# Word order behind the heads' products, and two steps that change places

## The chip, the cores and the metric

The kernel runs on one core of one Trainium2 chip. The metric is device time in microseconds of that core, first to last, of one execution; lower is better. A run's time is the median of several executions. A profile is one further execution, recorded by the hardware profiler.

The core has a matrix engine (TensorE, PE in the profile; its weight loads are shown as PEld), VectorE (DVE), ScalarE (ACT), GpSimd (POOL) and SyncE (SP). Each runs its own list of instructions in the order in which they were written, and waits for the others by semaphores. DMAs are issued here from SP and POOL.

## The reference

One layer of a decoder: normalise the rows of x, project them to q, k, v and a gate, do stick-breaking attention with 32 heads, gate, project back, add x, normalise again. `SEQ` is 256 rows, `D_MODEL` 4096, in float32.

```python
xn = rms_norm(h, norm_attn)
proj = xn @ w_in                      # (256, 4096) @ (4096, 16384)
q, k, v, g = split(proj, 4)
z = q @ k.T / sqrt(128)               # per head, strictly causal
log_a = log_sigmoid(z) + suffix_sum(log_sigmoid(-z))
o = exp(log_a) @ v
h = h + (o * silu(g)) @ w_out         # (256, 4096) @ (4096, 4096)
out = rms_norm(h, final_norm)
```

The two projections are nearly all of the arithmetic, and they read 320 MB of weights.

## The kernel before

**Products in three parts.** A float32 number is split into a high and a low part that TensorE can take; a product of two such matrices is then three matmuls, high by high, high by low, low by high, all into one PSUM bank. Such a *triple* is what `mm3` issues: 128 x 128 stationary by 128 x 512 moving, three times. The high part of a weight is a copy on ACT (`wh` in the profile), the low part is the difference on DVE (`wl`).

**Units and steps.** The work is cut into 20 *units*: 0 to 15 for the input projection (each gives the columns of two heads), 16 to 19 for the output projection. A unit has 16 *steps*; a step takes 256 of the 4096 inputs, two raw weight tiles of 512 KB loaded by SP.

**Eight or seven products.** A step is a 2 x 2 by 2 x 2 block product. Units 0 and 16 are plain, of eight triples a step. In the others a step has either eight triples (`EIGHT_PARTS`) or, by a scheme of the Strassen kind, seven (`SEVEN_PARTS`). A step of seven needs sums of weight blocks: POOL issues two accumulating DMAs for one of them (`add_block`), and DVE makes the others in place (`sums`: rows `raw<-raw,raw` and `raw<-raw`), before ACT and DVE split the results. In the profile a step of eight gives DVE two operations `wl<-raw,wh` of 128 x 1024; a step of seven three of these, one `wh<-raw,wh` of 128 x 512 and three sums. The low part of the third part of a step of seven (part 2, counted from 0) can be made only after the sums.

Which steps are of seven is in two lists:

```python
SEVEN = (1, 2, 4, 5, 7, 8, 10, 11, 13, 14)      # units 1 to 15
SEVEN_OUT = (1, 2, 4, 5, 7, 10, 11, 13, 14)     # units 17 to 19
```

In the last unit, 19, steps 11, 13 and 14 are of eight in any case, and its order is 0, 1, 3, 2, 4, 6, 5, 13, 7, 9, 8, 14, 10, 11, 12, 15. The stationary side has forms to match, built once (`new_forms`, `sums_of`, `blocks_of_heads`): six or seven blocks for the units 17 to 19, from the heads' outputs, which are read back from DRAM (`p<-spill`) for the steps of seven.

**Heads.** While a unit of the input projection runs, the two heads of the unit before are computed: transposes, scores, a scan by a triangular matrix, and the product with v. These are small matmuls, issued in bursts by `ten` between the triples (ten bursts a unit; tiles `tr`, `z`, `o`). `ten` sets a counter, `since_others`, to zero; each triple adds one.

**The order of the words.** `mm3` lets the 512 columns of a matmul be read and written in an order other than 0 to 511: four rounds, and in each every fourth group of columns, groups of eight words ("e") or of four ("c"). It is the same arithmetic. Three letters give the orders of a triple's matmuls. The seven triples behind a burst take theirs from `BEHIND_OTHERS`; after those, the first triple of a step takes `cce` (even steps) or `ecc` (odd), and all others `eee`.

**The last units.** In units 17 to 19 DVE and ACT also finish the blocks of the unit before: `block_out` loads a piece of x, adds it (`h<-h,xres`, DVE), squares the sum (`sq<-h`, ACT; this is an activation and a second instruction that reads its accumulated sum), and multiplies by the final norm's weights (`h<-h,grow`, DVE, in `gain_on`). There are four such pieces a unit.

**What sets the order.** No order is written by hand. `Plan` runs every piece of work through a list of planned events: a request for an engine has a cost and a key (a due time, in PE's time: `place_at`, `first`), and whenever an engine is free in the plan, the waiting request with the lowest key is written next. An engine is never left idle in the plan when something is ready. What is written is then fixed: on the chip each engine follows it. The wrapper's one line calls every instruction, so that the profile gives nearly all of them line 131, and tiles tell them apart.

Of the kernel before, what the change touches and what calls it, by code (L numbers as in the profile page):

```python
# [33 lines left out]

ROUNDS = 4
RUNS = {"e": 8, "c": 4}
BEHIND_OTHERS = ("ccc", "ecc", "eee", "cce", "eee", "eee", "ecc")
IN_STEP = ("cce", "ecc")
WARM, IDLE = 10, 640

# [3 lines left out]


SEVEN = (1, 2, 4, 5, 7, 8, 10, 11, 13, 14)
SEVEN_OUT = (1, 2, 4, 5, 7, 10, 11, 13, 14)
SOONER = 1.5
LATE, LATE_ADD = 1600, 2200
RAW_BUFS = 7  # L50
# [12 lines left out]
HEADS_AHEAD = 0  # L63
SUMS_LATER = 2
H_LATER = 6
ON_SCALAR = ((1, 3, 5), (1, 3))
AHEAD, SUMS_AHEAD = 6.0, 3.0
BLOCKS_LATER = 2
# [179 lines left out]
def kernel(  # L248
# [41 lines left out]
    for u, (kind, w, cols) in enumerate(units):  # L290
        for s in (step_at(u, k) for k in range(NS)):
# [3 lines left out]
            else:  # L295
                which = SEVEN_PARTS if s in (SEVEN if u < OUT0 else SEVEN_OUT) and not (u == LAST and s in EIGHT_LAST) else EIGHT_PARTS
            for i, (k, place, prods) in enumerate(which):
# [23 lines left out]
    def place_at(u, s):  # L321

        return place_of[u + int(s // NS), step_at(u + int(s // NS), int(s % NS))]
# [5 lines left out]
    def dve(emit, n, key=None, more=0, **kw):  # L329
        n = n if isinstance(n, tuple) else (n,)  # L330
        cost = sum(vector_ns(m) for m in n) + 122 * (len(n) - 1) + more
        return nc.work("vector", cost, emit, soon() if key is None else key, **kw)

    def act(emit, n, key=None, **kw):
        n = n if isinstance(n, tuple) else (n,)
        cost = sum(scalar_ns(m) for m in n) + 100 * (len(n) - 1)
        return nc.work("scalar", cost, emit, soon() if key is None else key, **kw)
# [169 lines left out]
    def new_forms(i, what):  # L507
        n = len(SEVEN_FORMS if i in (SEVEN if what == "s" else SEVEN_OUT) else EIGHT_FORMS)
        h = sp.tile([P, n, P], F32R, tag=f"xh{i}", name=f"{what}h{i}")
        l = sp.tile([P, n, P], F32R, tag=f"xl{i}", name=f"{what}l{i}")  # L510
        forms[i] = h, l
        return h, l
# [7 lines left out]
    def differences(i, y, key):  # L520

        y4 = y.rearrange("p (a b) c -> p a b c", a=KT)
        yield dve(
            lambda: nc.vector.tensor_tensor(
                out=y4[:, :, 0, :], in0=y4[:, :, 0, :], in1=y4[:, :, 1, :], op=ALU.subtract
            ),
            2 * P, key,
        )
        yield from both_parts(i, slice(4, 6), y4[:, :, 0, :], key)

    def sums_of(i, y, what, key):

        tt = nc.vector.tensor_tensor
        if i not in (SEVEN if what == "n" else SEVEN_OUT):
            yield from differences(i, y, key)
# [418 lines left out]
    def blocks_of_heads(s):  # L954
# [11 lines left out]
        key = min(place_at(OUT0, s + SUMS_LATER), place_of[OUT0 + 1, s] - 3e3)  # L966
        if s in SEVEN_OUT and s < NS - 1:
            nc.give("gh")
# [54 lines left out]
    def load_out(c, t):  # L1023
        pool, tag, bufs = (sp, "x" + "hl"[t] + str(LAST_STEPS[c - NJ + 4]), 1) if c >= NJ - 2 else (wp, "gh", ROWS)
        xres[c, t] = pool.tile([P, W], F32, tag=tag, name=f"xres{c}_{t}", bufs=bufs)
        return moved(
            "sync", lambda: nc.sync.dma_start(xres[c, t], x[t * P : (t + 1) * P, c * W : (c + 1) * W]), [W], soon(),
            after=lambda: nc.tell(("xres", c, t)),
        )

    def load_gain(c):
        grow[c] = wp.tile([P, W], F32, tag="gh", name=f"grow{c}", bufs=ROWS)
        return moved(
            "sync", lambda: nc.sync.dma_start(grow[c], gain_out[:, c * W : (c + 1) * W].partition_broadcast(P)), [W],
            soon(), after=lambda: nc.tell(("grow", c)),
        )

    def squares(c, t, place, cut, key=None):

        junk = att.tile([P, cut.stop - cut.start], F32, tag="att", name=f"sq{c}_{t}_{cut.start}")  # L1040
        yield act(
            lambda: nc.scalar.activation(
                junk, hs[c, t][:, cut], AF.Square, accum_out=ssq_h[:, t, place : place + 1]
            ),
            cut.stop - cut.start, key and key - 1e3,
        )

    ALL = slice(0, W)
# [1 line left out]
    def gain_on(c, t, key=None):  # L1050
        h = hs[c, t]
        yield nc.until(("grow", c))
        yield dve(lambda: nc.vector.tensor_tensor(out=h, in0=h, in1=grow[c], op=ALU.mult), W, key)

    def block_out(c, t, key):

        h = hs[c, t]
        yield nc.take("gh")
        yield load_out(c, t)
        yield nc.until(("xres", c, t))  # L1060
        yield nc.take("att")
        yield dve(lambda: nc.vector.tensor_tensor(out=h, in0=h, in1=xres[c, t], op=ALU.add), W, key)
        nc.give("gh")
        yield from squares(c, t, c, ALL, key)
        nc.give("att")
        yield from gain_on(c, t, key)

    def blocks_out(u, c):

        for d in range(2):  # L1070
            for t in range(NT):
                yield nc.until(("used", u, step_at(u, 2 * (NT * d + t))), ("C", u - 1))
                if t == 0:
                    yield nc.take("gh")
                    yield load_gain(c + d)
                key = place_at(u, 2 * (NT * d + t) + H_LATER)
                yield from block_out(c + d, t, key)
            nc.give("gh")
            nc.tell(("h", c + d))
# [74 lines left out]
    def part_done(c, t, place, cut, late):  # L1154
        yield nc.take("att")
        yield from squares(c, t, place, cut, late)
        nc.give("att")
        if place == NJ - 2:
            yield dve(lambda: mean_before_last(t), (NJ * NT, 64), late)
            nc.tell(("mean", t))  # L1160
        elif place == NJ - 1:
            yield nc.until(("mean", t))
            yield dve(lambda: joined(t), 64, late - 2)
            nc.tell(("most", t))
        else:
            yield nc.until(("most", t))
            yield from finish(c, t, late)
# [36 lines left out]
    def rows_out(c, t, f, key):  # L1204
        h = hs[c, t]
        if c >= NJ - 2:
# [6 lines left out]
            )  # L1213
        elif c in ON_SCALAR[t]:
            yield act(lambda: nc.scalar.activation(h, h, AF.Copy, scale=f), W, key)
# [21 lines left out]
    def product(n, k):  # L1237
# [4 lines left out]
        orders = "eee"  # L1242
        if since_others < len(BEHIND_OTHERS):
            orders = BEHIND_OTHERS[since_others]
        elif p["i"] == 0 and k == 0:
# [91 lines left out]
```

## Time and profile before

| | us |
|---|---|
| median of 3 runs | 1709.23 |
| lowest, highest | 1705.84, 1709.48 |
| profiled execution | 1706.34 |
| its span, first to last instruction | 1704.6 |
| granted TensorE clock, mean | 0.997 |

A page of a profile gives the busy time of each engine, the chain of work that ended last, the costliest groups of instructions, and DMA issues. A row of a timeline has the start, the length, the engine, the operation with what it writes and reads, and in brackets the idle time before it and what ended that. PE's matmuls are pipelined, so their lengths overlap; what counts is the distance from one start to the next. In a table of stretches a row has the length, then busy time and number of instructions of PE, PEld, DVE, ACT and POOL, the granted clock, the DMA engines' share and GB/s.

The stationary high parts of the input and output projections are `sh` and `oh`, the low ones `sl` and `ol`. A triple is `wh` by high, `wl` by high, `wh` by low.

### The profile page before, as it was taken

What the parts mean: (1) busy time and instruction counts of PE and PEld (TensorE: products, weight loads), DVE (VectorE), ACT (ScalarE), POOL (GpSimd) and SP (SyncE); (2) the same over time, 40 slices, a digit from 0 to 9 for tenths busy, and PEclk for the clock granted to TensorE, in tenths of its full rate; (3) what the DMA queues carried; (4) which work ended last, traced back from release to release, by engine and by line L of the source; (5) the groups of instructions that cost most, each with busy time, mean ns of one, the idle gap of its engine ahead of it and who ended that gap; (6) DMA issues with size and microseconds to landing.
All of it is one profiled execution on the core that took longest, in us unless ns stands there. A gap on an engine that the chain in (4) does not pass through costs nothing.

```text
span 1704.6 us, 25109 instructions
## 1 busy us (share of the span) xinstructions
PE 1685.6 (99%) x7776; PEld 1415.9 (83%) x7776; DVE 1607.4 (94%) x2025; ACT 1202.5 (71%) x1633; POOL 325.0 (19%) x400
## 2 busy tenths in 40 slices
PE   9999999999999999999999999999999999999996
PEld 7888888888888888888888888888888888888785
DVE  8889999999999999999999999999999977999997
ACT  8986767676767676767676768686767765666664
POOL 0012222222222222221212121212122112122110
PEclk9999999999999999999999999999999999999998
DMA  9968887979797878797978797878788977889795
GB/s 348 329 197 246 231 245 220 255 212 256 208 269 196 269 197 272 195 279 195 268 204 261 208 256 213 254 216 248 220 243 224 295 244 241 240 251 284 218 293 187
DMA packets 248439, 412.78 MB, mean 242 GB/s; under 512 B 28016, under 2 KB 72560, under 8 KB 248304
## 3 DMA queue, kind: packets, MB, share of 16 engines
q1 hardware_dynamic: 194544, 354.24, 62.2%
q0 software_dynamic: 53472, 56.65, 20.5%
q8 instruction: 61, 1.00, 0.2%
q14 instruction: 74, 0.61, 0.1%
q10 hardware_dynamic: 288, 0.28, 0.0%
HBM read 402.93 MB, written 8.13 MB: 241 GB/s over the span
## 4 chain that ended last, share of the span: by engine, by line
PE 94%; DVE 3%; issue 1%; DMA 1%; ACT 0%; SPq 0%; DVEq 0%; ACTq 0%
PE acc L131 90%; PE z L131 2%; PE o L131 2%; DVE wl L131 1%; PE tr L131 1%; DVE h L131 0%; DVE raw L131 0%; ACT wh L131 0%; DMA raw<-in_w_in_dram 0%; DMA raw<-in_w_out_dram 0%; DMA xres<-in_x_dram 0%; DVE wh L131 0%; DVE gv_sb L131 0%; SPq L131 0%; DVE scalars L131 0%
## 5 line engine op out<-in xcount | busy, mean ns | idle before, releaser
L131 ACT CAST wh<-raw 128x1024 fp32r<-128x1024 f32 (+1 forms) x989 | 918.2, 969 | 370.8 <-DVE raw L131 166.8
L131 DVE TENSOR_TENSOR wl<-raw,wh 128x1024 fp32r<-128x1024 f32 (+1 forms) x815 | 974.9, 1219 | 56.4 <-ACT wh L131 25.1
L131 PE MATMUL acc<-wh,sh 128*128 128x512 f32 x2048 | 774.3, 390 | 0.3 <-DVE sh L131 0.3
L131 PE MATMUL acc<-wh,sl 128*128 128x512 f32 x1898 | 727.9, 383 | 1.2 <-DVE sl L131 1.2
L131 PE MATMUL acc<-wl,sh 128*128 128x512 f32 x1748 | 669.0, 383 | 0.2 <-DVE wl L131 0.2
L131 POOL DMA_DIRECT2D raw<-in_w_in_dram x300 | 258.6, 957 | 1026.7 <-DMA raw<-in_w_in_dram 424.2
L131 PEld LDWEIGHTS acc<-wh,sh 128*128 128x128 f32 x2048 | 384.1, 188 | 78.0 <-PE acc L131 4.8
L131 PEld LDWEIGHTS acc<-wh,sl 128*128 128x128 f32 x1898 | 355.8, 187 | 67.2 <-DVE sl L131 1.8
L131 PEld LDWEIGHTS acc<-wl,sh 128*128 128x128 f32 x1748 | 328.3, 188 | 54.8 <-DVE wl L131 0.5
L131 DVE TENSOR_TENSOR raw<-raw,raw 128x512 f32<-128x512 f32 x348 | 237.5, 686 | 6.0 <-DMA raw<-in_w_out_dram 2.1
L131 PE MATMUL acc<-wh,oh 128*128 128x512 f32 x512 | 192.6, 384 | 0.6 <-DVE gv_sb L131 0.6
L131 PE MATMUL acc<-wh,ol 128*128 128x512 f32 x488 | 186.7, 383 | 0.0
L131 PE MATMUL acc<-wl,oh 128*128 128x512 f32 x464 | 177.7, 383 | 2.6 <-DVE wl L131 2.6
L131 DVE TENSOR_TENSOR wh<-raw,wh 128x512 fp32r<-128x512 f32 x174 | 119.3, 686 | 1.6 <-ACT wh L131 1.5
L131 DVE TENSOR_TENSOR raw<-raw 128x512 f32<-128x512 f32 x174 | 119.0, 684 | 0.0
L131 PEld LDWEIGHTS acc<-wh,oh 128*128 128x128 f32 x512 | 95.9, 187 | 18.0 <-DVE gv_sb L131 0.9
L131 PEld LDWEIGHTS acc<-wh,ol 128*128 128x128 f32 x488 | 91.5, 187 | 16.4
L131 PEld LDWEIGHTS acc<-wl,oh 128*128 128x128 f32 x464 | 87.0, 187 | 19.3 <-DVE wl L131 3.8
L131 POOL DMA_DIRECT2D raw<-in_w_out_dram x48 | 41.5, 968 | 181.4 <-DMA raw<-in_w_out_dram 78.7
L131 ACT ACTIVATE f<-f 128x384 f32<-128x384 f32 x96 | 50.5, 526 | 3.0
L131 POOL DMA_DIRECT2D p<-spill x27 | 17.5, 692 | 86.5 <-DVE ol L131 44.1
L131 DVE SCALAR_TENSOR_TENSOR gv_sb<-acc,scalars,gv_sb 128x512 f32<-128x512 f32 x45 | 33.5, 744 | 0.0
(83 smaller groups left out, 755.4 us busy)
## 6 DMA issues: line engine op xcount, KB each, us to landing
raw<-in_w_in_dram SPq DMA_DIRECT2D x1024, 256.0 KB, 4.3
raw<-in_w_out_dram SPq DMA_DIRECT2D x256, 256.0 KB, 4.5
raw<-in_w_in_dram POOLq DMA_DIRECT2D x300, 128.0 KB, 5.1
p<-spill POOLq DMA_DIRECT2D x27, 256.0 KB, 4.5
raw<-in_w_out_dram POOLq DMA_DIRECT2D x48, 128.0 KB, 5.1
xr<-in_x_dram SPq DMA_DIRECT2D x16, 256.0 KB, 5.5
xres<-in_x_dram SPq DMA_DIRECT2D x16, 256.0 KB, 6.2
out_dram<-h SPq DMA_DIRECT2D x16, 256.0 KB, 2.8
```

Of the source, the lines that this page charges most:

```text
L131: return self.tc.keep_in_program_order(getattr(self.engine, name)(*args, **kw))
```

## The change

Four edits.

- `BEHIND_OTHERS`: triples four and seven behind a burst. The fourth goes from `cce` to `eee`, the seventh from `ecc` to `cce`. Triples one (`ccc`), two (`ecc`), three, five and six (`eee`) stay.
- `SEVEN_OUT`: in units 17 to 19 step 4 becomes one of eight products, step 8 one of seven. The number of steps of each kind stays. With the steps go the form of the stationary blocks of steps 4 and 8, the accumulating DMAs, and the second reading of a step's heads' outputs.
- `GAIN_LATER`: the multiplication by the final norm's weights in `block_out` gets a key that is 8 us later. The last block pair, which multiplies in another place, isn't touched.
- `squares`: the planner's cost of a square is now that of two operations, of the piece's columns and of 64, instead of one. The instruction is the same.

```diff
-BEHIND_OTHERS = ("ccc", "ecc", "eee", "cce", "eee", "eee", "ecc")
+BEHIND_OTHERS = ("ccc", "ecc", "eee", "eee", "eee", "eee", "cce")
...
-SEVEN_OUT = (1, 2, 4, 5, 7, 10, 11, 13, 14)
+SEVEN_OUT = (1, 2, 5, 7, 8, 10, 11, 13, 14)
...
+GAIN_LATER = 8.0
...
             lambda: nc.scalar.activation(
                 junk, hs[c, t][:, cut], AF.Square, accum_out=ssq_h[:, t, place : place + 1]
             ),
-            cut.stop - cut.start, key and key - 1e3,
+            (cut.stop - cut.start, 64), key and key - 1e3,
         )
...
         yield from squares(c, t, c, ALL, key)
         nc.give("att")
-        yield from gain_on(c, t, key)
+        yield from gain_on(c, t, key + GAIN_LATER * 1e3)
```

## The prediction

> **What bounds the kernel.** I read the page first, then the three last units as stretches of time, then the timeline of TensorE (PE), then that of VectorE (DVE) before each place where PE stood still.
>
> ```profile
> span 1704.6 us, 25109 instructions
> PE 1685.6 (99%) x7776; PEld 1415.9 (83%) x7776; DVE 1607.4 (94%) x2025; ACT 1202.5 (71%) x1633; POOL 325.0 (19%) x400
> PE 94%; DVE 3%; issue 1%; DMA 1%; ACT 0%; SPq 0%; DVEq 0%; ACTq 0%
> ```
>
> PE has work in 99% of the span and carries 94% of the chain that ended last, so a change counts only if it shortens PE's row: by an idle stretch, or by the spacing of its 7158 matmuls of 512 columns. DVE at 94% is next, and is late first.
>
> ```profile
> 1449.80:1528.40 78.60, 78.60 (x358) 66.86 (x357) 75.90 (x93) 50.56 (x64) 13.79 (x16) 1.00 0.84 253
> 1528.40:1610.30 81.90, 79.58 (x359) 66.77 (x358) 78.46 (x94) 50.08 (x64) 16.65 (x20) 1.00 0.87 253
> 1610.30:1691.90 81.60, 81.10 (x367) 68.28 (x365) 72.62 (x100) 46.98 (x65) 7.45 (x9) 1.00 0.68 219
> ```
>
> These are units 17, 18 and 19 (length, then PE's busy time and instructions, then the other engines; PE's clock is 1.00). Units 17 and 18 hold the same 119 products, but 18 takes 3.3 us more and PE idles 2.3 us in it; in unit 19 it idles 0.5 us. PE's timeline has the places:
>
> ```profile
> 1554.85 0.40 PE L131 MATMUL acc<-wh,oh 128*128 128x512 f32 x1
> 1555.49 0.50 PE L131 MATMUL acc<-wl,oh 128*128 128x512 f32 x1 [0.24 <-DVE wl L131]
> 1555.83 0.40 PE L131 MATMUL acc<-wh,ol 128*128 128x512 f32 x1
> ...
> 1585.26 0.40 PE L131 MATMUL acc<-wh,oh 128*128 128x512 f32 x1
> 1587.74 0.49 PE L131 MATMUL acc<-wl,oh 128*128 128x512 f32 x1 [2.08 <-DVE wl L131]
> ...
> 1632.12 0.39 PE L131 MATMUL acc<-wh,oh 128*128 128x512 f32 x1
> 1632.77 0.48 PE L131 MATMUL acc<-wl,oh 128*128 128x512 f32 x1 [0.26 <-DVE wl L131]
> ```
>
> Starts are what to compare; undisturbed matmuls start 0.22 us apart (below). The first place is step 5 of unit 18 (0.64 + 0.34 - 0.44 = 0.54 us lost), the second step 11 of unit 18 (2.48 - 0.22, and some 0.1 at the next matmul as at the first place: 2.37), the third step 4 of unit 19 (0.65 - 0.22 + 0.1: 0.53). Together 3.44 us. All three are steps of seven products waiting for `wl` of a part that DVE makes from sums; the first and third follow a step of seven directly, and in the second a norm weight is multiplied just ahead of the sums.
>
> **Steps 4 and 8.** What a step costs DVE, from the groups of units 17 and 18, and the accumulating loads' landing time from the page:
>
> ```profile
> L131 DVE TENSOR_TENSOR wl<-raw,wh 128x1024 fp32r<-128x1024 f32 x79 | 92.6, 1218 | 1.7 <-ACT wh L131 1.5
> L131 DVE TENSOR_TENSOR raw<-raw,raw 128x512 f32<-128x512 f32 x34 | 23.2, 686 | 1.5 <-DMA raw<-in_w_out_dram 1.3
> L131 DVE TENSOR_TENSOR raw<-raw 128x512 f32<-128x512 f32 x17 | 11.6, 684 | 0.0
> L131 DVE TENSOR_TENSOR wh<-raw,wh 128x512 fp32r<-128x512 f32 x17 | 11.6, 684 | 0.9 <-ACT wh L131 0.9
> L131 DVE TENSOR_TENSOR h<-h,grow 128x512 f32<-128x512 f32 x8 | 5.5, 686 | 1.6 <-ACT sq L131 1.6
> raw<-in_w_out_dram POOLq DMA_DIRECT2D x48, 128.0 KB, 5.1
> ```
>
> A step of seven takes DVE 3 x 1.22 + 2 x 0.69 + 2 x 0.68 = 6.4 us and PE 7 x 3 x 0.22 = 4.62 us: DVE falls 1.8 us behind. A step of eight takes DVE 2 x 1.22 = 2.44 us and PE 5.28 us: DVE gains 2.84 us. The count of both kinds stays, so do the products, the accumulating loads of POOL's queue, SP's loads and the reloads of the heads' outputs; they move from step 4 to step 8. The forms are built in unit 16, where PE waits for none of this; I put them at 0.
>
> In unit 18 step 5 then follows two steps of eight (3 and 4) instead of a step of seven, so DVE has 1.8 + 2.84 = 4.6 us more before it, and it lacked 0.54: all of that goes. In unit 19, in its order 0, 1, 3, 2, 4, 6, 5, 13, 7, 9, 8, step 4 becomes one of eight itself and the stall of 0.53 has no place left; step 8 lies between steps 9 and 14, both of eight. In units 17 and 18 step 8 now follows step 7, a pair of sevens as 1 and 2 are. What is late next is DVE at steps 8 and 11 there. Ends: 0, and 1.8 + 2.84 = 4.6 us a unit if no lead is left. I take 0: unit 17 has four such pairs in its 78.60 us and PE never idles, and the 4.6 us that step 4 no longer takes lies ahead of step 8.
>
> **Norm weights later.** DVE before the second place:
>
> ```profile
> 1576.10 3.50 DVE L131 TENSOR_TENSOR wl<-raw,wh 128x1024 fp32r<-128x1024 f32 x3 [0.63 <-ACT wh L131]
> 1579.52 0.68 DVE L131 TENSOR_TENSOR h<-h,xres 128x512 f32<-128x512 f32 x1
> 1581.05 0.69 DVE L131 TENSOR_TENSOR h<-h,grow 128x512 f32<-128x512 f32 x1 [0.85 <-ACT sq L131]
> 1581.66 0.69 DVE L131 TENSOR_TENSOR wh<-raw,wh 128x512 fp32r<-128x512 f32 x1
> 1582.26 1.41 DVE L131 TENSOR_TENSOR raw<-raw,raw 128x512 f32<-128x512 f32 x2
> 1583.59 1.22 DVE L131 TENSOR_TENSOR wl<-raw,wh 128x1024 fp32r<-128x1024 f32 x1
> 1585.33 4.62 DVE L131 TENSOR_TENSOR wl<-raw,wh 128x1024 fp32r<-128x1024 f32 x4
> ```
>
> DVE runs in the planner's order. It stood 0.85 us for ACT's square, then multiplied (0.61 to the next start), and only then made the sums (1582.26), whose `wl` is the second or third from 1585.33. The edit gives that multiply a due time 8 us later and charges the planner for the square's second instruction, so sums that are ready go first: 1.46 us sooner. The `wl` of step 12 at 1583.59 was written before the late one only because the sums, and ACT's copy of them, were late; without that another 1.14 us or more goes. The sums' own load must have landed:
>
> ```profile
> 1574.69 1.73 POOL L131 DMA_DIRECT2D raw<-in_w_out_dram  x2 [2.30 <-DMA raw<-in_w_out_dram]
> ```
>
> 5.1 us after the second issue is about 1580.7, ahead of 1582.26. Ends: 0 (the planner, which fills DVE with whatever is ready, keeps the order) and 2.37. I take 2.0, nearer the upper end, since 1.46 + 1.14 covers it. Behind the delayed multiply wait the release of two row buffers and the next block's load, which have steps to spare; in unit 19 the last such multiply comes before the final additions, and I put it at 0 (upper end 0.69, one multiply among them).
>
> **Words in groups.** The page cannot tell groups of four from groups of eight, but the sequence of the kernel's products is known, so each start in PE's timeline has its order. After the heads' products PE falls into one of two paces:
>
> ```profile
> 184.50 0.39 PE L131 MATMUL acc<-wh,sh 128*128 128x512 f32 x1
> 188.65 0.39 PE L131 MATMUL acc<-wh,sh 128*128 128x512 f32 x1
> ...
> 1431.27 0.39 PE L131 MATMUL acc<-wl,oh 128*128 128x512 f32 x1
> 1431.51 0.39 PE L131 MATMUL acc<-wh,ol 128*128 128x512 f32 x1
> 1431.74 0.39 PE L131 MATMUL acc<-wh,oh 128*128 128x512 f32 x1
> 1435.88 0.39 PE L131 MATMUL acc<-wh,oh 128*128 128x512 f32 x1
> ...
> 1558.13 0.38 PE L131 MATMUL acc<-wh,oh 128*128 128x512 f32 x1
> 1558.81 0.39 PE L131 MATMUL acc<-wh,oh 128*128 128x512 f32 x1
> 1559.05 0.39 PE L131 MATMUL acc<-wl,oh 128*128 128x512 f32 x1
> 1559.28 0.38 PE L131 MATMUL acc<-wh,ol 128*128 128x512 f32 x1
> 1561.92 0.38 PE L131 MATMUL acc<-wh,ol 128*128 128x512 f32 x1
> ...
> 129.27 0.38 PE L131 MATMUL acc<-wh,sh 128*128 128x512 f32 x1
> 129.94 0.38 PE L131 MATMUL acc<-wh,sh 128*128 128x512 f32 x1
> ```
>
> The first two rows are the starts of triples four and ten of a slow group: 18 matmuls in 4.15 us, 0.230 each. 1431.74 and 1435.88 are the same of the last one: 4.14 us. There are eleven such groups, and nine slow ones that end after triple five. Quick pace: 1559.28 to 1561.92 is 12 matmuls in 2.64 us, 0.220 each. So triples four to nine cost a slow group 4.15 - 3.96 = 0.19 us too much.
>
> What ends the slow pace shows after the first stall. At 1558.13 PE is slow; two matmuls in fours come (step 6 begins with `cce`), then three in eights 0.23 to 0.24 apart, then eights follow and from 1559.28 PE is quick. A slow group runs the same way to the end of triple three (pair of fours, then three eights 0.23 to 0.24 apart: 1431.27, 1431.51, 1431.74), but then the old triple four brings fours, and the slow pace stays. The new triple four has eights. So I expect the quick pace from triple four on: 11 x 0.19 = 2.1 us, and 9 x 5 x 0.009 = 0.4 us. Two quick cases cancel: 37 groups pay for the fours of triple four as at 129.27 (three matmuls in 0.67, 0.01 too much: 0.4 us saved), and 38 groups may pay as much at triple seven or the next step's fours. The stalls' own slow stretch (15 matmuls from 1555.83 to 1559.28 in 3.45, 0.15 too much, once for each stall of unit 18) goes with the stalls: 0.3. Ends for the words: +0.5 (slow groups stay, quick ones pay) and -3.0. I take -2.5, by the one place where the sequence occurs.
>
> [...]
>
> **Sum.** 0.54 + 2.0 + 0.53 + 0.3 + 2.5 = 5.9 us. The profiled execution took 1706.34 us (1.7 outside its span), so one like it would take 1700.4. The median of the runs shown, 1709.23, is 2.9 above it; I carry that over: 1703.3 us, 0.35% less. What a measurement can tell is 0.2%, 3.4 us: faster is below 1705.8, slower above 1712.6.
>
> **Rivals.**
> *The order at step 11 stays.* The planner may find nothing else ready and multiply as early as before. Then 2.0 and half of the 0.3 are missing: 1705.4. For it: DVE at 1579.52 took the block's addition, with a later due time than sums would have. Against: the 0.85 us of idling.
> *The words do nothing.* The slow pace is set by something else than triple four, or returns with it: 3.4 us remain, 1705.8. For it: only one place shows the exit. [...]
> *Steps 7 and 8 empty DVE's lead (slower).* In units 17 and 18 the pair takes 4.6 us that step 4 no longer does, but a lead is bounded by the buffers, and what step 4 saved may already be lost at step 8. Step 11 then waits up to 4.6 us longer in each: 9.2 - 1.1 - 0.2 - 2.5 = 5.4 us more, 1714.6. It decides from 7.2 us of new waits on; less gives no change. For it: unit 18 idles at a step 11 already. Against: the two steps of eight, 3 and 4, and one, 9, on either side.
>
> **How the numbers follow.** All as summed 0.55; order stays 0.15; words nothing 0.14; lead lost 0.11; other mixtures 0.05. Faster: 0.53 of the first, 0.10 of the second, 0.06 of the third, 0.69. Slower: the fourth and 0.02 of the rest, 0.13. Same: 0.18. The range goes from 1699.5 (all upper ends, 3.44 + 0.3 + 3.0 below a run like the profiled one) to 1709.0, which takes in the second and third, alone or joined (1707.9). The first alone has 1699.5 to 1705.5.
>
> **What would show it.** Unit 18 as long as unit 17 within 0.5 us, and no PE idling on `wl` at its steps 5 and 11 or at step 4 of unit 19. In DVE's timeline the multiply by `grow` behind `raw<-raw,raw` of the next step of seven. After the heads' products, 18 matmuls from triple four in 3.96 to 3.98 us in every group, and no group at 4.15. It is wrong if PE idles at step 8 or 11 of units 17 and 18, or if slow groups remain.

## The result, and the profile after

The changed kernel takes 1702.31 us (median of 7 runs, 1701.33 to 1705.52); the kernel before, run beside it, 1708.99 (7 runs, 1705.84 to 1710.1). The ratio is 0.9965 with a 95% interval from 0.9954 to 0.9977: faster, by more than the 0.2% that a measurement can tell. The profiled execution took 1701.40 us against 1706.34, which is 4.94 less; predicted were 5.9 less and a median of 1703.3.

From the page of the changed kernel, its span, the engines' busy times and the chain that ended last (the new line in the file moves line 131 to 132):

```profile
span 1699.7 us, 25128 instructions
PE 1682.8 (99%) x7776; PEld 1416.8 (83%) x7776; DVE 1606.3 (95%) x2025; ACT 1203.5 (71%) x1633; POOL 325.2 (19%) x400
PE 93%; DVE 3%; DMA 2%; issue 1%; ACT 0%; SPq 0%; DVEq 0%; ACTq 0%
```

and its three last units as stretches of time, with the columns of the prediction's table:

```profile
1447.50:1526.20 78.70, 78.70 (x359) 66.97 (x359) 75.32 (x91) 50.30 (x64) 15.61 (x18) 1.00 0.86 262
1526.20:1606.40 80.20, 79.20 (x359) 66.77 (x358) 77.95 (x95) 50.93 (x65) 15.70 (x20) 1.00 0.85 252
1606.40:1687.70 81.30, 81.29 (x367) 68.39 (x365) 74.24 (x103) 46.83 (x65) 8.42 (x11) 1.00 0.73 225
```

PE is still the bound. Unit 17 is as long as before, unit 18 is 80.2 us instead of 81.9, unit 19 is hardly shorter. From the first start of each unit in PE's timeline, and to the last matmul's start:

| us | before | after | gained |
|---|---|---|---|
| ahead of unit 17 | 1449.78 | 1447.53 | 2.25 |
| unit 17 | 78.63 | 78.64 | 0.0 |
| unit 18 | 81.87 | 80.22 | 1.65 |
| unit 19 | 80.98 | 80.91 | 0.07 |
| last matmul's start to the span's end | 13.34 | 12.41 | 0.93 |

The sum is 4.90. PE's timeline of the changed kernel, behind the burst that the prediction took for its slow group, and at step 11 of unit 18:

```profile
184.04 0.39 PE L132 MATMUL acc<-wl,sh 128*128 128x512 f32 x1
184.27 0.39 PE L132 MATMUL acc<-wh,sl 128*128 128x512 f32 x1
184.50 0.38 PE L132 MATMUL acc<-wh,sh 128*128 128x512 f32 x1
184.72 0.38 PE L132 MATMUL acc<-wl,sh 128*128 128x512 f32 x1
...
188.47 0.38 PE L132 MATMUL acc<-wh,sh 128*128 128x512 f32 x1
...
1582.65 0.40 PE L132 MATMUL acc<-wh,oh 128*128 128x512 f32 x1
1584.05 0.49 PE L132 MATMUL acc<-wl,oh 128*128 128x512 f32 x1 [1.00 <-DVE wl L132]
1584.38 0.38 PE L132 MATMUL acc<-wh,ol 128*128 128x512 f32 x1
```

Triple three ends the slow pace (0.23 and 0.23 apart), and from triple four's first matmul, 184.50, the next is 0.22 away; the 18 matmuls from triple four take 3.97 us instead of 4.15. Over the 50 groups behind bursts in which these 18 can be read (49 before), eleven lay above 4.1 us before and none does now; one, near 114 us, stays slow up to triple seven and takes 4.07. At step 11 of unit 18 PE still idles: 1.40 + 0.33 - 0.44 = 1.29 us lost, where it was 2.37. The stalls at step 5 of unit 18 and at step 4 of unit 19 are gone. The waits of PE from unit 17 on, added up in the trace of before and of after (total, times, longest):

```profile
PE acc L131 <- DVE wl L131: 2.6, 3, 2.1
```

```profile
PE acc L132 <- DVE wl L132: 1.0, 1, 1.0
```

VectorE ahead of that one stall, in the changed kernel:

```profile
1574.01 0.69 DVE L132 TENSOR_TENSOR h<-h,xres 128x512 f32<-128x512 f32 x1
...
1579.83 0.69 DVE L132 TENSOR_TENSOR raw<-raw,raw 128x512 f32<-128x512 f32 x1
1580.43 0.69 DVE L132 TENSOR_TENSOR h<-h,grow 128x512 f32<-128x512 f32 x1
1581.03 0.69 DVE L132 TENSOR_TENSOR raw<-raw 128x512 f32<-128x512 f32 x1
1581.63 5.77 DVE L132 TENSOR_TENSOR wl<-raw,wh 128x1024 fp32r<-128x1024 f32 x5
```

The multiply by the norm weights, which the prediction expected behind the sums, still stands among them. Only the idle 0.85 us ahead of it is gone.

### The profile page after: what moved, and what is told of

Same layout as the page of the kernel before. It is cut to its first block, busy times and chain, and to the rows that moved or that the text cites. A ratio compares the mean times of both kernels' runs of the same rounds, so it can differ in the third digit from the quotient of the medians.

```text
span 1699.7 us, 25128 instructions
## 1 busy us (share of the span) xinstructions
PE 1682.8 (99%) x7776; PEld 1416.8 (83%) x7776; DVE 1606.3 (95%) x2025; ACT 1203.5 (71%) x1633; POOL 325.2 (19%) x400
## 4 chain that ended last, share of the span: by engine, by line
PE 93%; DVE 3%; DMA 2%; issue 1%; ACT 0%; SPq 0%; DVEq 0%; ACTq 0%
PE acc L132 88%; PE z L132 2%; PE o L132 2%; DVE wl L132 1%; DMA raw<-in_w_out_dram 1%; DVE h L132 1%; PE tr L132 1%; DMA xres<-in_x_dram 1%; DVE raw L132 0%; DMA raw<-in_w_in_dram 0%; SPq L132 0%; ACT wh L132 0%; DVE gv_sb L132 0%; ACT sq L132 0%; DVE scalars L132 0%
```

## The experiments

Three sets; each is compared with runs of the kernel before beside it on the same chip (medians 1707.24 of 28 runs, 1707.19 of 21, 1708.16 of 10): words, plan, steps and norm weights alone are the first, the triples and words with steps the second. "Lost" is start spacing above 0.22 us, with the next matmul's excess.

### Words alone, and the plan alone

```diff
 words_only: the kernel before with
+BEHIND_OTHERS = ("ccc", "ecc", "eee", "eee", "eee", "eee", "cce")
 plan_only: the changed kernel with the old words
+BEHIND_OTHERS = ("ccc", "ecc", "eee", "cce", "eee", "eee", "ecc")
```

> Only the order of the words is changed; steps, norm weights and the planner's cost stay as before. Theory (triple four in eights ends the slow pace): 2.2 us less than before (range 1.8 to 2.8), unit 17 begins near 1447.5 us instead of 1449.8, every group behind the heads' products takes 3.96 to 3.98 us for the 18 matmuls of triples four to nine, and the three stalls of units 18 and 19 stay (0.5, 2.4, 0.5 us, give or take 0.3). Rival (the order does nothing; units 1 to 16 shortened for another reason): within 0.5 us of before.

> Steps 4 and 8, the later norm weights and the square's cost are changed; the words stay as before. Theory: the two parts add, so this takes what words_only leaves of the whole difference of 6: 3 to 4 us less than before by the time, 2.7 us by the span of one profile. Units 1 to 16 as before (unit 17 begins near 1449.8), slow groups stay. Rival (the parts depend on each other, since the words shift when the heads' products end): the sum of words_only and plan_only misses the whole difference by over 1.5 us.

Words alone: 1705.32 us (11 runs), ratio 0.9987 (0.9978 to 0.9996). No group lies above 4.1 us, unit 17 starts 1.26 us sooner than in the profile of before, and the three stalls stand as they were:

```profile
PE acc L131 <- DVE wl L131: 2.7, 3, 2.2
```

Plan alone: 1703.80 us (11 runs), ratio 0.9978 (0.9969 to 0.9987). Eleven groups lie above 4.1 us, as before; step 11 of unit 18 loses 1.50 and a new wait at its step 0 loses 0.4; the end is 0.95 shorter. So both halves do something by themselves, 1.9 and 3.4 us, and the product of the two ratios is 0.9965, that of the whole change.

### Which triple

```diff
 triple_four: the kernel before, fourth triple alone
-"cce"
+"eee"
 triple_seven: the kernel before, seventh triple alone
-"ecc"
+"cce"
 no_seven: the changed kernel, seventh triple in eights
-"cce"
+"eee"
```

> Only triple four goes from cce to eee; triple seven stays ecc and the rest is as before. Theory (triple four's fours keep the slow pace alive): all of the words' part is here, 2.2 us less than before (1.7 to 2.8), no slow group from triple four on. Rival (it is triple seven, or the two together): under 0.7 us less, groups of 4.15 us remain.

> Only triple seven goes from ecc to cce; triple four stays cce and the rest is as before. Theory: slow groups stay slow through triple six, 18 matmuls in 4.0 to 4.2 us, and the time is within 0.8 us of before. Rival (triple seven carries the gain): 1.5 us less or better.

> The changed kernel, but with triple seven in eights too, so fours only in triples one and two. Theory: no slow group is left for triple seven to end; its fours cost a quick group 0.013 us or nothing, so this is within 0.7 us of the changed kernel, at most 0.5 us better. Rival (triple seven ends slow groups that triple four leaves): groups of 4.1 us or longer come back and it takes 1 us more than the changed kernel or worse.

Triple four alone: 1706.18 us, ratio 0.9990 (0.9981 to 0.9999), no group above 3.98 us, unit 17 starts 2.77 us sooner. By the medians that is 1.0 us, less than the 1.7 to 2.8 that I expected. Triple seven alone: 1708.00, ratio 1.0001 (0.9992 to 1.0009), and its unit 17 starts at the time of before. It isn't without effect on the groups: none lies above 4.1 us, seven take 4.08 to 4.09, so the slow groups become shorter, but the quick ones pay for the fours at both places (3.97 or 3.99). The changed kernel with eights in triple seven: 1701.45 (5 runs), ratio 0.9963 (0.9951 to 0.9976), groups 3.960 us on average against 3.970 in the changed kernel. Triple four carries the words' gain; beside it, fours in triple seven buy nothing.

The profiles of triple four alone and of triple seven alone show something more at step 11 of unit 18. PE's timeline with triple seven alone:

```profile
1585.30 0.40 PE L131 MATMUL acc<-wh,oh 128*128 128x512 f32 x1
1587.79 0.49 PE L131 MATMUL acc<-wl,oh 128*128 128x512 f32 x1 [2.09 <-DVE wl L131]
...
1588.81 0.50 PE L131 MATMUL acc<-wh,ol 128*128 128x512 f32 x1
1589.11 0.63 PE L131 MATMUL acc<-wh,oh 128*128 128x512 f32 x1
1589.54 0.63 PE L131 MATMUL acc<-wl,oh 128*128 128x512 f32 x1
...
1592.10 0.52 PE L131 MATMUL acc<-wl,oh 128*128 128x512 f32 x1
1592.46 0.39 PE L131 MATMUL acc<-wh,ol 128*128 128x512 f32 x1
```

and the stretch behind the stall, with the granted clock in the third column from the end, first of this kernel, then of before:

```profile
1588.00:1592.00 4.00, 4.00 (x12) 3.16 (x12) 3.96 (x6) 0.00 (x0) 0.00 (x0) 0.62 1.05 396
```

```profile
1587.70:1592.00 4.30, 4.26 (x19) 3.51 (x20) 4.26 (x6) 0.00 (x0) 0.00 (x0) 1.00 1.00 351
```

One microsecond after PE resumes, the clock falls, to a mean of 0.62 from 1588.00 to 1592.00, and matmuls start 0.43 us apart until 1592.10. From 1588.81 to 1592.46 are nine spacings in 3.65 us, at 0.23 each 2.07: 1.6 us lost. Before and the words alone have a stall of about the same length (2.08 and 2.23 us of idling) and no such row: from the second matmul behind it they start 0.23 to 0.24 apart, in before with the clock at 1.00. Unit 18 is 83.66 us long here, 83.40 with triple four alone (which has the same row of matmuls 0.43 apart), 81.87 before.

### Steps alone, norm weights alone

```diff
 steps_only: the kernel before with
-SEVEN_OUT = (1, 2, 4, 5, 7, 10, 11, 13, 14)
+SEVEN_OUT = (1, 2, 5, 7, 8, 10, 11, 13, 14)
 gain_only: the kernel before with
+GAIN_LATER = 8.0
+            (cut.stop - cut.start, 64), key and key - 1e3,
+        yield from gain_on(c, t, key + GAIN_LATER * 1e3)
 words_and_steps: the changed kernel without these last three lines
```

> Only step 4 of eight and step 8 of seven; norm weights, cost and words as before. Theory as predicted (each part removes its own stalls): the stalls at step 5 of unit 18 and step 4 of unit 19 go, the one at step 11 of unit 18 stays near 2.4 us: 1 to 1.5 us less than before. Rival (the norm weights' later due time does nothing good; the steps' change alone reorders VectorE): the stall at step 11 shrinks to 1 us or less here too, and the time is 2.5 to 5 us less than before, as good as or better than plan_only.

> Only the norm weights 8 us later and the square's cost; steps and words as before. Theory as predicted: the stall at step 11 of unit 18 falls from 2.4 us to 0.4, the other two stay, 1.5 to 2 us less than before. Rival (the later multiply is only put ahead of other sums, in units 17 and 19 too): the stall at step 11 falls to 1 us or less, but new ones of 0.5 to 2 us come in units 17 and 19, and the time is from 1 us less to 2 us more than before.

> The words and the steps of the change, without the later norm weights and without the square's cost. Theory as predicted (the later norm weights remove 2.0 us at step 11): 1 to 2 us slower than the changed kernel. Rival (they bring nothing once the steps are moved): as fast as the changed kernel or up to 2 us faster, and the stall at step 11 of unit 18 at or below its 1.29 us there.

Steps alone: 1702.20 us (6 runs, 1701.55 to 1703.59), ratio 0.9970 (0.9958 to 0.9981). Unit 18 is 79.46 us, step 11 loses 0.54, and there is no other stall; the end is 11.89 us instead of 13.34. That is five microseconds by medians for the edit that I had put at one. VectorE and TensorE of this kernel at the place of the old stall:

```profile
1574.75 0.68 DVE L131 TENSOR_TENSOR h<-h,grow 128x512 f32<-128x512 f32 x1
...
1580.82 0.68 DVE L131 TENSOR_TENSOR h<-h,xres 128x512 f32<-128x512 f32 x1
...
1582.62 4.62 DVE L131 TENSOR_TENSOR wl<-raw,wh 128x1024 fp32r<-128x1024 f32 x4
1587.16 0.68 DVE L131 TENSOR_TENSOR h<-h,grow 128x512 f32<-128x512 f32 x1
```

```profile
1586.16 0.52 PE L131 MATMUL acc<-wl,oh 128*128 128x512 f32 x1 [0.23 <-DVE wl L131]
```

With no due time touched, the last piece's multiply (1587.16) already stands behind the late `wl` (1584.89, the third of the four from 1582.62): the steps alone did what I expected of the norm weights.

Norm weights and square alone: 1706.77 us, ratio 0.9997 (0.9988 to 1.0006), no change that can be told, as the rival had it. Step 11 of unit 18 loses only 1.08, but PE now also waits at step 14 of unit 17 (0.89), at step 5 of unit 18 (1.09) and at step 1 of unit 19 (1.14). The waits of PE added up, and VectorE ahead of step 11:

```profile
PE acc L132 <- DVE wl L132: 3.0, 4, 0.9
```

```profile
1581.98 0.69 DVE L132 TENSOR_TENSOR h<-h,xres 128x512 f32<-128x512 f32 x1
1583.53 0.69 DVE L132 TENSOR_TENSOR h<-h,grow 128x512 f32<-128x512 f32 x1 [0.85 <-ACT sq L132]
1584.13 0.68 DVE L132 TENSOR_TENSOR raw<-raw,raw 128x512 f32<-128x512 f32 x1
```

The total of the waits is larger than before (3.0 against 2.6), and the order that I wanted broken stands: addition, 0.85 us for the square, multiply, and only then the sums.

Words and steps together, without norm weights and square: 1701.12 us (5 runs), ratio 0.9959 (0.9947 to 0.9972). Its profile has step 11 at 0.53 us lost, unit 18 at 79.37, the end at 11.88. The last two edits are not needed for the gain.

### Due time or square, and the best of it

```diff
 sparse_and_steps: the kernel before with
+BEHIND_OTHERS = ("ccc", "ecc", "eee", "eee", "eee", "eee", "eee")
+SEVEN_OUT = (1, 2, 5, 7, 8, 10, 11, 13, 14)
 key_added: the changed kernel without the square's cost
 square_added: the changed kernel without GAIN_LATER
 after_again: the changed kernel
```

> Steps as in the changed kernel, words in fours in triples one and two alone, norm weights and square as before. Theory (triple four carries the words' gain, triple seven carries nothing; the steps carry the rest; the later norm weights cost about a microsecond on top of them): ratio to the kernel before 0.9955 to 0.9962, not distinguishable from words_and_steps (0.9959), and not above the changed kernel of this job; no group of 18 matmuls over 4.0 us; PE idle at step 11 of unit 18 about 0.5 us. Rival (triple seven's fours are needed at the units' ends): slower than words_and_steps by 0.1% or more, with a slow stretch after the first step of a group.

> The changed kernel without the square's second instruction in the planner's costs: words, steps and the later due time of the norm weights. Theory (the later due time itself is what costs, since it moves the multiply in every block and makes another wait late): lost time at step 11 of unit 18 about 1.0 to 1.5 us as in the changed kernel (1.29), against 0.53 without it; ratio 0.9960 to 0.9968. Rival (the square's cost in the planner does it, the due time is harmless): step 11 loses about 0.5 us and the ratio is that of words_and_steps, 0.9959 or less.

> The changed kernel with the norm weights' due time as before: words, steps and the square's cost. Theory (the due time costs, the square's cost does little): step 11 of unit 18 loses about 0.5 us, ratio 0.9955 to 0.9962. Rival (the square's cost does it): step 11 loses 1.0 to 1.5 us, ratio 0.9960 to 0.9968.

> The changed kernel as it is, beside the three others on one chip, so that their medians can be compared. Theory (the later norm weights and the square's cost are a loss on top of the steps): slower than sparse_and_steps by 0.5 to 1.5 us. Rival (no loss, the earlier difference of 1.2 us was between chips): within 0.3 us of it.

| one chip | median us (range) | ratio (95%) | lost at step 11, unit 18 |
|---|---|---|---|
| sparse_and_steps | 1700.01 (1699.30 to 1700.72) | 0.9955 (0.9941 to 0.9968) | 0.52 |
| square_added | 1700.78 (1699.67 to 1702.20) | 0.9959 (0.9947 to 0.9972) | 0.75 |
| after_again | 1701.63 (1700.62 to 1703.45) | 0.9965 (0.9952 to 0.9977) | 1.55 |
| key_added | 1702.28 (1701.93 to 1704.55) | 0.9971 (0.9959 to 0.9982) | 0.91 |

The due time costs something; the square's cost isn't seen to. Every run of key_added (6) is slower than every run of sparse_and_steps (5). These two differ in triple seven as well, which by no_seven changes little; key_added and square_added, which differ in nothing else but these two edits, overlap by 0.3 us. The traces are clearer: at step 11 the five profiles with the steps and the due time lose 0.91 to 1.55 us, the four with the steps and without it 0.52 to 0.75. The profile of key_added has the stall at step 11 a little smaller than the changed kernel's, and a second one, 1.26 us lost, at step 1 of unit 19; so my expectation that step 11 alone shows it was too narrow:

```profile
PE acc L132 <- DVE wl L132: 1.6, 2, 1.0
```

Where the due time acts is seen in VectorE with the square's cost alone, to be held against the changed kernel's rows above:

```profile
1578.89 0.68 DVE L131 TENSOR_TENSOR h<-h,xres 128x512 f32<-128x512 f32 x1
...
1580.70 4.63 DVE L131 TENSOR_TENSOR wl<-raw,wh 128x1024 fp32r<-128x1024 f32 x4
1585.24 0.69 DVE L131 TENSOR_TENSOR h<-h,grow 128x512 f32<-128x512 f32 x1
```

Unit 18 has four such pieces. Without the due time the third is multiplied at 1572.83 and the fourth added at 1578.89 and multiplied at 1585.24, behind the late `wl`. With it (the changed kernel) the third is multiplied at 1565.93 already, and so the fourth is added at 1574.01 and multiplied at 1580.43, ahead of that `wl`. An edit that was to make the multiply later made it sooner, and in the four other profiles with the steps and the due time it did the same. How the planner comes to take the third piece sooner was not followed further.

The best version is sparse_and_steps, the changed kernel with eights in triple seven and without the due time and the square's cost. It is 1.6 us below the changed kernel by medians, with ranges that overlap by 0.1 us; by the intervals of the two ratios the difference isn't certain.

## Why the prediction was right

The forecast was faster by 5.9 us, and the time lies in its range, but the mechanism held only in part. By the prediction's own signs, three things are not as told: unit 18 is 1.6 us longer than unit 17 instead of at most 0.5, PE still idles at step 11 of unit 18, and the multiply by `grow` isn't behind the sums. That the total came so near is in part luck.

**Words (predicted 2.5, and by one place in the trace).** The mechanism is as told: the slow groups leave the slow pace with triple three and are quick from triple four on, all but the one near 114 us. In the four profiles with both old triples, ten to fifteen groups lie above 4.1 us; in the nine with the new triple four, none. Unit 17 starts 2.25 us sooner in the profile of after. In the nine profiles with the new triple four it starts 0.75 to 2.8 us sooner than before, in the four others with the old one between 1.2 later and 0.4 sooner, so one profile is good to about a microsecond. The least, 0.75, is a second profile of the changed kernel, in which PE loses 0.6 to 0.7 us each near 1020 and 1105 us, where the first loses nothing. By the medians, words alone are worth 1.9 us and triple four alone 1.0. The quick groups' 0.4 and -0.4 cancel as told: fours cost a quick group 0.013 us, at triple four before and at triple seven now (3.973 and 3.974 against 3.960 with eights at both). So triple seven is a small loss, if anything. Against the rival that the words do nothing stands the interval of words alone, 0.9978 to 0.9996.

**Steps 4 and 8 (predicted 0.54 and 0.53).** Both small stalls went, and the pair of steps 7 and 8 made no wait above 0.1 us of its own without the due time (with it, the second profile of the changed kernel loses 0.39 at step 8). But the term was far too small: steps alone take 1.82 us from the stall at step 11 (2.36 to 0.54) and 1.45 from the end, besides 0.53 from each small stall, and the sum had nothing for the first two. It isn't the 4.6 us of lead that does it at step 11, since step 8 takes back what step 4 gave. At the end of the `wl` that PE waits for there, VectorE has made the same number of low parts (768 from the kernel's start), high parts, sums and additions in both kernels. What differs is the order that the planner wrote. VectorE gets there 1.2 us sooner after the start of unit 17 (136.7 instead of 137.9): one multiply by the norm weights (0.6 us) is no longer ahead, and VectorE idles some 0.8 us less, since the two waits for ACT's square that unit 18 had before (0.79 and 0.85) are gone and new ones are shorter. PE needs the late `wl` at the sixth triple of the step instead of the fourth, 1.3 us later; and PE itself comes some 0.7 sooner, without the stall at step 5 and the slow stretch behind it. That gives 1.2 + 1.3 - 0.7 = 1.8 us. The prediction looked for a new order only in the edit of the norm weights; moving two steps reorders the rest as well.

**Norm weights later (predicted 2.0 of the 2.37).** This is the step that failed. "Sums that are ready go first" is not what the planner did: the multiply stayed ahead of them in the kernel with the norm weights alone, 0.85 us of idling included, and stayed among them in the changed kernel. Step 11 did lose 1.08 us less after the change, but the steps account for that, and the norm weights and the square together give back 0.76 (1.29 against 0.53 of words and steps). Step 11 loses 0.75 with the square's cost alone, so 0.54 of the 0.76 comes with the due time. The rival that the order stays had the place right; it was outweighed because the steps gave what it took away.

**Slow stretches (predicted 0.3) and unit 19.** The stretches behind the stalls went, but others came. PE's timeline near the start of unit 19 of the changed kernel:

```profile
1609.05 0.39 PE L132 MATMUL acc<-wh,oh 128*128 128x512 f32 x1
1609.28 0.39 PE L132 MATMUL acc<-wl,oh 128*128 128x512 f32 x1
...
1612.51 0.39 PE L132 MATMUL acc<-wh,oh 128*128 128x512 f32 x1
1612.73 0.38 PE L132 MATMUL acc<-wl,oh 128*128 128x512 f32 x1
```

From 1609.05 to 1612.51 are 15 spacings in 3.46 us, 0.231 each, with no idle time in the trace. In all, 61 of the unit's 366 matmuls are slow and cost 0.59 us, before 24 and 0.18: 0.4 of the 0.53 gained is lost again. In unit 18 the slow matmuls cost 0.27, before 0.42. So 0.3 predicted became 0.15 - 0.41, a loss of 0.26. What starts the slow pace here was not tried. In the four kernels with the steps and without the due time, unit 19's slow matmuls cost 0.17, 0.18, 0.32 and 0.40 us, in the five with it 0.28 to 0.59, so the due time is not shown to be the cause.

**The end (predicted 0, upper end 0.69).** It is 0.93 shorter. VectorE scales the first row half between the last matmuls and the second half's last square. The chain of waits of before and of after:

```profile
1690.43 3.67 DVE h L131 x8
...
1694.19 0.07 ACT sq L131
```

```profile
1686.02 3.17 DVE h L132 x7
1689.19 0.08 DVE scalars L132
...
1689.29 0.07 ACT sq L132
```

The last matmul starts at 1691.26 before and at 1687.30 after. The square comes 2.93 us behind it before and 1.99 after: VectorE starts this run of pieces 1.3 us ahead of the last matmul instead of 0.8, and it has seven of them left instead of eight. That VectorE is less late because of its new order is my reading; no run changes the end alone. With either the steps or the norm weights and square alone the end is 11.89 us, 1.45 less.

**The sum.** 2.25 (words) + 1.65 (unit 18) + 0.07 + 0.93 = 4.90 in the profiles against 5.9. Units 18 and 19 were to gain 3.4 (0.54 + 2.0 + 0.53 + 0.3) and gained 1.72; the words fell short by 0.25, and the end brought 0.93 that was not in the sum. Two errors of opposite sign nearly met, and that is luck: steps, norm weights and square were to save 0.54 + 0.53 + 2.0 = 3.07 us and saved 0.53 + 0.53 + 1.08 + 0.93 = 3.07, though the steps alone save 4.3 and the due time gives some of it back. The medians differ by 6.7, more than the profiles: the last section has a possible reason.

## What to carry to other kernels

Where a greedy planner writes the order, an edit that moves some work reorders the rest: compare the late engine's list up to the next stall and to the end of the kernel before another edit is credited with them. A due time in such a planner is not a place in an order: a later one may bring the work sooner, so look at the order that results, and try each edit without its companions; here one of three worked against the other two. If a pace outlasts its cause, look for the first spot that ends it in the trace and bring that pattern closer.

## What the runs showed of the hardware

In two of four profiles a wait of PE of 2.1 us cost more than its length. With PE idle for 2.07 to 2.23 us at step 11 of unit 18, the matmuls from the second one behind it started 0.23 to 0.24 us apart in before (granted clock 1.00) and with the words alone; with triple seven alone (granted clock 0.62 from 1588.00 to 1592.00) and with triple four alone a row of them started 0.43 apart. It begins 1.0 and 0.8 us after PE resumed, and its nine spacings take 3.65 and 3.64 us instead of 2.07, 1.6 us more in each. Behind the waits at the same step in the changed kernel (1.0 us), with the plan alone (1.2) and in key_added (1.0) no such row follows. What brings such a row, and why in two of the four profiles, no run shows.

A fall in some executions alone would also fit the spread of the kernel before. Of its 59 runs in the three sets, the 20 with a mean granted clock of 0.995 or 0.996 have a median of 1708.5, the 13 with 0.998 one of 1706.6. Of the 33 runs of words, triple four and triple seven alone, which have that stall too, seven are at 0.996, and none lower; of the 66 runs of the nine kernels whose waits in the last units are 1.3 us or less, three. That the slower runs of before owe their time to this place is not shown, since only profiled executions have a trace; if they do, shortening the stall saves more than the stall in some executions.
